# Down projection of an encoder block: operand parts kept in item order, a fresh accumulator for the last product, three weight loads traced earlier, the last block's products moved to VectorE

## The chip, the core and the metric

The kernel runs on one core of one Trainium2 chip. A core has a matrix engine (TensorE, PE in the profile, with PEld for its weight loads), VectorE (DVE), ScalarE (ACT), GpSimd (POOL) and a queue engine (SyncE, SP, SPq for its DMA issues). Matrix products land in an accumulator memory (PSUM), everything else is worked on in SBUF. The metric is the device time of one execution in microseconds (us). Time before: 1780.49 us, the median of 3 runs (1779.59 to 1781.81).

## The reference

One encoder layer is applied to two token groups of 256 and 512 tokens (768 rows of 1024 channels in all), with the same weights and in float32. Three token mixers (a state-space model, a differential attention, a cross-attention) are merged and projected, and a gated feed-forward network follows. Only its last line matters here:

```
h2 = rmsnorm(x, ffn_norm_g[li])
g, up = jnp.split(h2 @ w_gate_up[li], 2, axis=-1)
x = x + (jax.nn.silu(g) * up) @ w_down[li]
```

`w_gate_up` is 1024 x 5632, `w_down` is 2816 x 1024. The last matrix product, (768 x 2816) by (2816 x 1024), and the addition to `x` are the down projection.

## The kernel before

**Three matmuls for one.** A float32 operand is split into a high part (ScalarE copies it to a rounded format) and a low part (VectorE subtracts the high part from the original). `mm3` (lines 748 to 753) then issues three matmuls: high by high, high by low, low by high. `split_evac` (line 739) makes the two parts of an operand; with a `scale` it multiplies on the way.

**The blocks ahead of the down projection.** The hidden dimension is worked off in 11 feature blocks `fb` of 256 columns, each with a "gate" and an "up" half (`block`, line 1437). A block makes seven products of half size (Strassen-Winograd form), each of 12 matmuls on 384 columns; `plus` adds products up on VectorE, and a `fin` finishes each of four output quarters: `fin_gate` (tanh on ScalarE, then VectorE) or `fin_up`, which multiplies the gate by the up value. `fin_up` runs on GpSimd in these blocks (`kw`, line 1463). `hid_store` (line 1425) writes the finished hidden block to DRAM (`hid_scr`). `hook` is called only in the last "up" block, right after its first product is copied; it is `down_early`, which loads and prepares the first operands of the down projection.

**The down projection** is again a Strassen-Winograd product, over halves of the tokens (`r`, 384 rows), of the hidden dimension (`kh`) and of the output columns (`f`, 512 wide). It has seven products in the order P2, P1, P5, P6, P3, P7, P4. Each is cut into NG = 6 granules along the hidden dimension, five of two 128-row slices and one of a single slice. A pair (product, granule) is an item; there are 42, numbered from 0 (P2 is items 0 to 5, P1 6 to 11, P5 12 to 17, and so on). An item of two slices has 18 matmuls of 512 columns (three token tiles of 128 rows, two slices, three matmuls each), the single-slice item 9, and a product 99. Per item:

- `w_fetch(i)` brings the weights. P2, P3 load a quarter of `w_down` into a raw buffer (`dwr`), P1 into one of six long-lived tiles `ch[g]` (`dch` in the profile), all on the SP queue. P5, P6 and P4 work on `ch[g]` too: a GpSimd DMA adds another quarter to it in place (line 1752). P7 loads `dwt` tiles and adds a quarter to them in the same way.
- `a_load` (line 1725) brings hidden values from `hid_scr` (`da`), again on SP. Twelve of them, for the two quarters that P5 to P7 use, are asked for at P5's items.
- `make(i)` turns them into parts: the weights' high and low part (`whd` line 742, `wld` line 743), for P5, P6, P3 and P7 an addition or subtraction of two hidden quarters (`tt`, recorded at line 1765, the subtraction of P5 in place in `da`), and the token operand's high and low part (`dxh` line 745, `dxl` line 746). Four buffers hold weight parts and three hold token parts.
- then the item's matmuls, and after a product's last item three additions of the accumulators into the residual rows `x1` (line 1840, `x<-x,dn`), and for some products the store of the finished rows.

The loop makes item i + 2 before the matmuls of item i, fetches weights six and hidden values seven items ahead.

**Accumulators.** Tiles in two groups of PSUM buffers, "d" (five) and "b" (three). P2 has three fresh d tiles, P1 three fresh b tiles, P5 three fresh d tiles. P6, P7 and P4 go on adding to P1's b tiles and P3 to P5's d tiles: the Winograd chain sums are made in PSUM. So the first matmul of P4 on a tile comes after P7's addition has read that tile.

**What sets the order.** Instructions are traced in program order, but the queue of each engine is put in order by a planner that simulates the kernel at build time: an instruction goes to its engine when the planner believes its inputs to be there. The waits on the chip are semaphores that follow data and buffers, and an engine takes its queue in order. `pin`, that is `keep_in_program_order`, fixes an instruction behind the one traced just before it on the same engine (whatever that is, pinned or not). Before, the down projection's loads on SP and its adding loads on GpSimd are pinned, and nothing on ScalarE and VectorE is.

Of the kernel before, what the change touches and what calls it, by code (L numbers as in the profile page):

```python
# [8 lines left out]
F32 = mybir.dt.float32  # L9
F32R = mybir.dt.float32r  # L10
I32 = mybir.dt.int32
AF = mybir.ActivationFunctionType
# [614 lines left out]
def hybrid_block(ctx, tc, A, outs, consts):  # L627
    nc = tc.nc
    v, act, gp, pe = nc.vector, nc.scalar, nc.gpsimd, nc.tensor
    mul, add, sub = ALU.mult, ALU.add, ALU.subtract  # L630
# [17 lines left out]
    def uid(s):  # L648
        cnt[0] += 1
        return f"{s}_{cnt[0]}"  # L650
# [85 lines left out]
    def mean_eps(x, n, d):  # L736
        v.tensor_scalar(out=x, in0=x, scalar1=1.0 / d, scalar2=1e-6, op0=mul, op1=add)

    def split_evac(hi, lo, src, scale=None):

        if scale is None:
            act.activation(hi, src, AF.Copy)
            v.tensor_tensor(out=lo, in0=src, in1=hi.bitcast(F32), op=sub)  # L743
        else:
            act.activation(hi, src, AF.Copy, scale=scale)
            v.scalar_tensor_tensor(out=lo, in0=src, scalar=scale, in1=hi.bitcast(F32), op0=mul, op1=sub)  # L746

    def mm3(ps, wh, wl, xh, xl, start, stop, more=False):

# [47 lines left out]
    def bcast_load(pool, ap, n, name):  # L797
        t = pool.tile([128, n], F32, name=name)
        nc.sync.dma_start(t, ap.unsqueeze(0).to_broadcast([128, n]))
        return t  # L800
# [168 lines left out]
    D, P3 = {}, {}  # L969
    mrs2 = k1.tile([128, 4], F32, name="mrs2")  # L970
    with tc.tile_pool(name="nrm", bufs=1) as pool, tc.tile_pool(name="nrmg", bufs=1) as pg:
# [4 lines left out]
        ps = env.psa("gT")  # L976
# [9 lines left out]
        for t0 in (0, 2):  # L986
            for k0 in range(0, 8, 2):
                ps = env.psb("nT")
# [16 lines left out]
        for t in range(4):  # L1005

            tc.keep_in_program_order(v.scalar_tensor_tensor(out=xm[t], in0=xm[t], scalar=1.0, in1=xm[t], op0=mul,
                                                            op1=mul, accum_out=mss[:, t : t + 1]))
# [6 lines left out]
        g = bcast_load(pg, A["norm_mix_g"][0], 1024, "gmix")  # L1015
# [84 lines left out]
    with ExitStack() as c2:  # L1100
# [4 lines left out]
        for c in range(12):  # L1105
            W.by_dma = True
            w = W.get()
            for m in range(2):
                M = 2 * c + m
                for sg, (c0, n) in enumerate(SEGS):  # L1110
                    gt = glp.tile([128, 512], F32, name=uid("glt"), tag="glt")
                    ps = psd("gl")
# [23 lines left out]
    for i, nme in enumerate(("diff_q_g", "diff_k_g")):  # L1136
        g = rp[:, 2, 64 * i : 64 * i + 64]
# [247 lines left out]
    with tc.tile_pool(name="gelu", bufs=1) as yp:  # L1385
        for m in range(2):
            gelu_load(m, yp)
        for j, h in enumerate(DIFF_HEADS):
# [3 lines left out]
            for n_v, u_ in enumerate(v_units(last // 2) if h is None else qk_units(h)):  # L1392
                n_unit += 1
                W.by_dma = n_unit >= LOADED and not final
                m, r = divmod(n_unit, GELU_UNITS)
# [4 lines left out]
                if final and n_v % 2:  # L1400

                    t = slice(128 * (n_v - 1), 128 * (n_v + 1))
# [24 lines left out]
    def new_block(what, fb):  # L1427
        if what == "gate":
            act_in[fb] = fa.tile([128, 2, TOK], F32, name=uid("fa"), tag="fa")
# [14 lines left out]
    def block(what, fb, hook=None):  # L1444

        new_block(what, fb)
        w = W.get()
        fin = fin_gate if what == "gate" else fin_up

        def prod(l, r):  # L1450
            ps = psd(what)[:, 0:HT]
            (wh, wl), (xh, xl) = w[l], R[r]
            for k in range(4):
                mm3(ps, wh[:, k], wl[:, k], xh[:, k], xl[:, k], k == 0, k == 3)
            return ps

        def plus(o, x, y):
            v.tensor_tensor(out=o, in0=x, in1=y, op=add)

        tmp = [stg.tile([128, TOK], F32, name=uid("fs"), tag="brr") for _ in range(2)]  # L1460
        h1, h2 = slice(0, HT), slice(HT, TOK)
        (c11, c12), (c22, c21) = ((t[:, h1], t[:, h2]) for t in tmp)
        kw = {} if what == "gate" else {"eng": gp}
        act.activation(c12, prod("A11", "B11"), AF.Copy)
        if hook:
            hook()
        plus(c11, c12, prod("A12", "B21"))
        fin(fb, c11, 0, h1, **kw)
        plus(c12, c12, prod("S2", "T2"))
        p5 = prod("S1", "T1")  # L1470
        plus(c21, c12, prod("S3", "T3"))
        plus(c22, c21, p5)
        plus(c12, c12, p5)
        fin(fb, c22, 1, h2, **kw)
        plus(c12, c12, prod("S4", "B22"))
        fin(fb, c12, 0, h2, **kw)
        plus(c21, c21, prod("A22", "T4"))
        fin(fb, c21, 1, h1, **kw)

    with ExitStack() as c5:  # L1480
# [64 lines left out]
        x1, XB, Z = L["x1"], L["XB"], L["Z"]  # L1545
        S = pair(XA, "s5o")
        for c in range(4):
            w = W.get()
            for m in range(2):
                M = 2 * c + m  # L1550
                t = gtp.tile([128, TOK], F32, name=uid("gt"), tag="glr")
                zs = stg.tile([128, TOK], F32, name=uid("zs"), tag="brr")
                gp.dma_start(zs, z_scr[M])
                for c0, n in SEGS:
                    ps = psd("glu")
# [18 lines left out]
        g = fnp.tile([128, 1024], F32, name="gffn", bufs=1)  # L1574
# [120 lines left out]
    P2, P1, P5, P6, P3, P7, P4 = range(7)  # L1695
    NG = NFB // 2 + 1

    def granule(kh, g):
        if g < NG - 1:
            return (NG - 1) * kh + g, 0, 2  # L1700
        return NFB - 1, kh, 1

    ITEMS = [(p, g) for p in range(7) for g in range(NG)]
    AHEAD, FETCH, LOAD = 2, 6, 7
    EARLY = 4
    pin = tc.keep_in_program_order
# [5 lines left out]
    DP, a_raw, ch, w_raw, parts = {}, {}, {}, {}, {}  # L1712
# [14 lines left out]
    def w_quarter(kh, f, g):  # L1727
        fb, m, n = granule(kh, g)
        return wd[:, 2 * fb + m : 2 * fb + m + n, 512 * f : 512 * f + 512]

    def w_fetch(i):

        if i >= len(ITEMS):
            return
        p, g = ITEMS[i]
        n = granule(0, g)[2]
        view = lambda t: t.rearrange("p (k c) -> p k c", k=2)[:, 0:n]
        acc = None
        if p in (P1, P5, P6, P4):
            if p == P1:  # L1740
                ch[g] = view(DP["ch"].tile([128, 1024], F32, name=f"dch{g}"))
                pin(nc.sync.dma_start(ch[g], w_quarter(0, 0, g)))
            else:
                acc = {P5: (0, 1), P6: (1, 1), P4: (1, 0)}[p]
            t = ch[g]
        else:
            t = view(DP["r"].tile([128, 1024], F32, name=f"dwt{i}", tag="dwt") if p == P7 else
                     W.praw.tile([128, W.HALF], F32, name=f"dwr{i}", tag="wr"))
            src, acc = {P3: ((1, 1), None), P7: ((0, 1), (1, 1)), P2: ((1, 0), None)}[p]
            pin(nc.sync.dma_start(t, w_quarter(*src, g)))  # L1750
        if acc:
            pin(gp.dma_start(t, w_quarter(*acc, g), accum_op=add))
        w_raw[i] = t

    def make(i):

        if i >= len(ITEMS):
            return
        p, g = ITEMS[i]
        n = granule(0, g)[2]  # L1760
        t = w_raw.pop(i)
        wh, wl = (x.rearrange("p (k c) -> p k c", k=2)[:, 0:n] for x in W.tiles(f"d{i}"))
        split_evac(wh, wl, t)
        A_ = lambda r, kh: a_raw[(r, kh), g]
        tt = lambda o, x, y, op: v.tensor_tensor(out=o, in0=x, in1=y, op=op)
        sign = 0.5
        s_ = A_(1, 0) if p in (P5, P6, P3, P7) else None
        if p == P1:
            x = A_(0, 0)
        elif p == P5:  # L1770
            x = s_
            tt(x, x, A_(1, 1), sub)
        elif p == P6:
            x = s_
            tt(x, x, A_(0, 0), sub)
        elif p == P3:
            x = DP["t"].tile([128, 2, HT], F32, name=uid("ds4"), tag="ds4")[:, 0:n]
            tt(x, s_, A_(0, 1), add)
        elif p == P7:
            x = s_  # L1780
            tt(x, x, A_(1, 1), add)
            sign = -0.5
        else:
            x = A_(*((0, 1) if p == P2 else (1, 1)))
        xh, xl = (da_f.tile([128, 2, HT], F32R, name=uid("dx" + w), tag="dx" + w)[:, 0:n] for w in "hl")
        split_evac(xh, xl, x, sign)
        parts[i] = xh, xl, wh, wl

    def item_loads(i):
# [19 lines left out]
    xbctx.close()  # L1809

    with ExitStack() as c7:
        for k, n in (("a", 1), ("ch", 1), ("t", 2), ("r", 3)):
            DP[k] = c7.enter_context(tc.tile_pool(name="down" + k, bufs=n))
        HOME = {P1: (0, 0, add), P5: (1, 1, add), P6: (0, 1, sub), P3: (0, 1, add), P7: (1, 1, sub),
                P2: (0, 0, add), P4: (1, 0, add)}
        acc = {}
        for i in range(EARLY, LOAD):
            item_loads(i)
        for i in range(AHEAD + 3, FETCH):
            w_fetch(i)  # L1820
        for i, (p, g) in enumerate(ITEMS):
            item_loads(i + LOAD)
            w_fetch(i + FETCH)
            make(i + AHEAD)
            bank = "b" if p in (P1, P6, P7, P4) else "d"
            if g == 0 and p in (P1, P5, P2):
                acc[bank] = [PS[bank].tile([128, 512], F32, name=uid("dn"), tag=bank) for _ in range(3)]
            ps = acc[bank]
            n = granule(0, g)[2]
            xh, xl, wh, wl = parts.pop(i)  # L1830
            for t in range(3):
                c = slice(128 * t, 128 * t + 128)
                for k in range(n):
                    mm3(ps[t], xh[:, k, c], xl[:, k, c], wh[:, k], wl[:, k],
                        g == 0 and k == 0 and p in (P1, P5, P2), g == NG - 1 and k == n - 1, p in (P6, P3, P7, P4))
            if g == NG - 1:
                r, f, op = HOME[p]
                for t in range(3):
                    o = x1[3 * r + t][:, 512 * f : 512 * f + 512]
                    v.tensor_tensor(out=o, in0=o, in1=ps[t], op=op)  # L1840
                    if p in (P1, P3, P7, P4):
                        nc.sync.dma_start(os_[3 * r + t][:, 512 * f : 512 * f + 512], o)
    de.close()
# [44 lines left out]
```

## Time and profile before

| what | value |
|---|---|
| median of 3 runs | 1780.49 us (1779.59 to 1781.81) |
| the profiled execution's own time | 1780.2 us |
| its span, first to last instruction | 1778.4 us |
| mean granted TensorE clock | 0.994 of full speed |
| PE busy, PE weight loads busy | 1747.6 us (98%), 1613.2 us (91%) |
| DVE, ACT, POOL busy | 1265.1, 888.0, 282.2 us |
| down projection's first and last matmul start | 1606.2 and 1773.9 us |

The profile is a page of one execution with the span cut into views: the list of waits (who waited for whom, in all, how often, the longest), stretches (busy time of every engine with the number of instructions, the granted TensorE clock and the share of the 16 DMA engines), and the timeline of an engine (start, duration, line, operation, output and inputs; in brackets the engine's idle time just before and what ended it). The granted clock is 1.00 at full speed. Busy time of PE alone says little, as its matmuls overlap; the pitch from start to start is what counts.

### The profile page before, as it was taken

To read this page: it belongs to the slowest core of one execution; us is meant where nothing else is said; L and a number is where in the kernel's file an instruction comes from. 1 tells how busy PE (TensorE), PEld (TensorE's weight loads), DVE (VectorE), ACT (ScalarE), POOL (GpSimd) and SP (SyncE) were. 2 spreads that over 40 slices of the span, in tenths; PEclk is the share of its full clock that TensorE was granted. 3 is DMA by queue.
4 is the path that set the end of the run, shared out by engine and by line. 5 is a ranking of instruction groups with operands and counts; after the bars stand their busy time and mean duration, and the time that the engine had idled before them with its cause. 6 is when DMAs were issued, how large, how long until landed. Compare 5 with 4: busy or idle time off the path is not lost.

```text
span 1778.4 us, 29418 instructions
## 1 busy us (share of the span) xinstructions
PE 1747.6 (98%) x11194; PEld 1613.2 (91%) x11194; DVE 1265.1 (71%) x2342; ACT 888.0 (50%) x1856; POOL 282.2 (16%) x300
## 2 busy tenths in 40 slices
PE   9999999999999999999989999999999999999998
PEld 9999988999999999999979888888889999997786
DVE  6765658699999689788866435353598777774874
ACT  6444434677676356877756434232343333343342
POOL 0000000000000101110110002000136565541211
PEclk9999999999999999999999999999999999999999
DMA  7222745655656466543773336331312333338865
GB/s 257 82 84 96 139 112 117 179 136 139 154 134 159 130 156 163 117 91 90 161 175 98 120 124 245 113 116 65 90 62 93 107 94 112 97 134 258 188 156 122
DMA packets 209661, 234.09 MB, mean 132 GB/s; under 512 B 57832, under 2 KB 173296, under 8 KB 209520
## 3 DMA queue, kind: packets, MB, share of 16 engines
q1 hardware_dynamic: 184080, 164.05, 30.5%
q0 software_dynamic: 24288, 65.02, 17.2%
q10 hardware_dynamic: 1152, 3.15, 0.5%
q8 instruction: 88, 1.44, 0.3%
q14 instruction: 53, 0.43, 0.1%
HBM read 165.78 MB, written 41.22 MB: 116 GB/s over the span
## 4 chain that ended last, share of the span: by engine, by line
PE 55%; DMA 4%; DVE 2%; issue 1%; SPq 1%; ACT 0%; POOL 0%; ACTq 0%; DVEq 0%; POOLq 0%
PE br L751 4%; PE br L752 4%; PE br L753 4%; PE gate L751 3%; PE gate L753 3%; PE up L753 3%; PE gate L752 3%; PE up L752 3%; PE up L751 3%; PE dn L753 2%; PE dn L751 2%; PE dn L752 2%; PE av L1311 2%; PE qk L752 2%; PE qk L751 2%; PE qk L753 2%
## 5 line engine op out<-in xcount | busy, mean ns | idle before, releaser
L595 ACT ACTIVATE wh<-wr 128x1024 fp32r<-128x1024 f32 x124 | 140.6, 1133 | 73.1 <-PE br L752 30.2
L601 DVE TENSOR_TENSOR wl<-wr,wh 128x1024 fp32r<-128x1024 f32 x82 | 108.5, 1325 | 84.8 <-ACT wh L595 82.9
L751 PE MATMUL gl<-Hhi,wh 128*128 128x256 f32 (+1 forms) x384 | 132.4, 345 | 2.3 <-ACT glt L1114 2.3
L753 PE MATMUL gl<-Hhi,wl 128*128 128x256 f32 (+1 forms) x384 | 129.0, 336 | 0.0
L752 PE MATMUL gl<-Hlo,wh 128*128 128x256 f32 (+1 forms) x384 | 128.7, 335 | 0.0
L752 PE MATMUL qk<-wl,Hhi 128*128 128x256 f32 x384 | 109.1, 284 | 0.0
L751 PE MATMUL qk<-wh,Hhi 128*128 128x256 f32 x384 | 108.8, 283 | 0.4 <-ACT V L1210 0.4
L753 PE MATMUL qk<-wh,Hlo 128*128 128x256 f32 x384 | 108.6, 283 | 0.0
L599 POOL DMA_DIRECT2D wl<-wr x42 | 36.6, 872 | 453.2 <-ACT wl L598 428.6
L752 PE MATMUL dn<-wld,dxh 128*128 128x512 f32 x231 | 90.6, 393 | 3.3 <-DVE wld L743 3.3
L751 PE MATMUL dn<-whd,dxh 128*128 128x512 f32 x231 | 90.7, 393 | 2.0 <-DVE x L1840 2.0
L753 PE MATMUL dn<-whd,dxl 128*128 128x512 f32 x231 | 89.8, 395 | 1.9 <-DVE dxl L746 1.9
L751 PEld LDWEIGHTS gl<-Hhi,wh 128*128 128x128 f32 x384 | 72.3, 188 | 9.7 <-ACT glt L1114 2.7
L753 PEld LDWEIGHTS gl<-Hhi,wl 128*128 128x128 f32 x384 | 72.0, 188 | 8.0
L752 PEld LDWEIGHTS gl<-Hlo,wh 128*128 128x128 f32 x384 | 72.2, 188 | 7.2
L1280 DVE TENSOR_REDUCE nm<-sc 128x1 f32<-128x512 f32 (+1 forms) x96 | 56.6, 598 | 28.0 <-PE sc L1275 27.0
L751 PEld LDWEIGHTS qk<-wh,Hhi 128*128 128x128 f32 x384 | 73.1, 190 | 1.5 <-ACT V L1210 0.6
L557 ACT ACTIVATE wh_S<-ws 128x512 fp32r<-128x512 f32 x70 | 41.1, 626 | 65.5 <-PE up L752 36.9
L753 PEld LDWEIGHTS qk<-wh,Hlo 128*128 128x128 f32 x384 | 73.3, 191 | 0.3
L752 PEld LDWEIGHTS qk<-wl,Hhi 128*128 128x128 f32 x384 | 72.8, 190 | 0.6
L558 DVE TENSOR_TENSOR wl_S<-ws,wh_S 128x512 fp32r<-128x512 f32 x70 | 57.9, 851 | 15.9 <-ACT wh_S L557 15.9
L1282 ACT ACTIVATE p<-sc,nm 128x512 f32<-128x512 f32 (+1 forms) x96 | 59.1, 620 | 17.5 <-DVE nm L1280 17.0
(478 smaller groups left out, 6016.5 us busy)
## 6 DMA issues: line engine op xcount, KB each, us to landing
wr<-in_w_in_dram SPq DMA_DIRECT2D x48, 512.0 KB, 4.6
wr<-in_w_gate_up_dram SPq DMA_DIRECT2D x44, 512.0 KB, 3.5
wl<-wr POOLq DMA_DIRECT2D x42, 512.0 KB, 5.2
wr<-in_w_branch_dram SPq DMA_DIRECT2D x24, 512.0 KB, 3.9
glr<-gl_scr POOLq DMA_DIRECT2D x24, 384.0 KB, 3.5
hid_scr<-fa SPq DMA_DIRECT2D x11, 768.0 KB, 6.3
wr<-in_w_mem_kv_dram SPq DMA_DIRECT2D x16, 512.0 KB, 3.6
wr<-in_w_in_dram SPq DMA_DIRECT2D x32, 256.0 KB, 4.7
```

What stands on the lines that cost most here:

```text
L557: self.nc.scalar.activation(f(hi), src, AF.Copy)
L558: self.nc.vector.tensor_tensor(out=f(lo), in0=src, in1=f(hi).bitcast(F32), op=ALU.subtract)
L595: self.nc.scalar.activation(hi, r, AF.Copy)
L599: self.nc.gpsimd.dma_start(lo, r.bitcast(F32R), accum_op=ALU.add)
L601: self.sub.tensor_tensor(out=lo, in0=r, in1=hi.bitcast(F32), op=ALU.subtract)
L751: pe.matmul(ps, wh, xh, start=start, stop=False, **kw)
L752: pe.matmul(ps, wh, xl, start=False, stop=False, **kw)
L753: pe.matmul(ps, wl, xh, start=False, stop=stop, **kw)
L1280: v.tensor_reduce(out=nm[:, m : m + 1], in_=ps, axis=AX.X, op=ALU.max, negate=True)
L1282: act.activation(pm[:, 0:n], ps, AF.Exp, bias=nm[:, m : m + 1], accum_out=s1s[:, tt : tt + 1] if m == 0 else s2)
L1311: pe.matmul(po[:, 0:128], aT[:, 128 * k : 128 * k + 128], V[:, c0 // 128 + k, 128 * (h % 2) : 128 * (h % 2) + 128], start=(k == 0), stop=( ...
```

## The change

Five edits, all but the last two lines within the down projection and its lead-in:

1. `split_evac` takes a `pin`, and `make` pins all that it issues on ScalarE and VectorE: weight parts, sums of hidden quarters, token parts.
2. P4 gets three fresh d tiles (`FRESH`) and no longer adds to the b chain. To make up for it, P7's end adds each b tile to a second set of residual rows as well (`o2`): three more VectorE additions.
3. The weight loads of P1's first three granules (items 6 to 8) are traced before the hidden loads of items 4 to 6 and are not pinned; later ones stay where they were, pinned.
4. The pools of the down projection are opened in another order (`ch` last), so `ch` lies on other memory that was used before it.
5. In the last "up" block (the one with a hook) `fin_up` runs on VectorE, not on GpSimd.

```
-    def split_evac(hi, lo, src, scale=None):
+    def split_evac(hi, lo, src, scale=None, pin=lambda i: i):
         if scale is None:
-            act.activation(hi, src, AF.Copy)
-            v.tensor_tensor(out=lo, in0=src, in1=hi.bitcast(F32), op=sub)
+            pin(act.activation(hi, src, AF.Copy))
+            pin(v.tensor_tensor(out=lo, in0=src, in1=hi.bitcast(F32), op=sub))
...
-        kw = {} if what == "gate" else {"eng": gp}
+        kw = {} if what == "gate" or hook else {"eng": gp}
...
-                pin(nc.sync.dma_start(ch[g], w_quarter(0, 0, g)))
+                load = nc.sync.dma_start(ch[g], w_quarter(0, 0, g))
+                if g > 2:
+                    pin(load)
...
-        split_evac(wh, wl, t)
+        split_evac(wh, wl, t, pin=pin)
-        tt = lambda o, x, y, op: v.tensor_tensor(out=o, in0=x, in1=y, op=op)
+        tt = lambda o, x, y, op: pin(v.tensor_tensor(out=o, in0=x, in1=y, op=op))
...
-        split_evac(xh, xl, x, sign)
+        split_evac(xh, xl, x, sign, pin)
...
-        for k, n in (("a", 1), ("ch", 1), ("t", 2), ("r", 3)):
+        for k, n in (("a", 1), ("t", 2), ("r", 3), ("ch", 1)):
...
+        FRESH = (P2, P1, P5, P4)
         acc = {}
+        for i in range(NG, NG + 3):
+            w_fetch(i)
         for i in range(EARLY, LOAD):
             item_loads(i)
...
-            w_fetch(i + FETCH)
+            if i + FETCH >= NG + 3:
+                w_fetch(i + FETCH)
             make(i + AHEAD)
-            bank = "b" if p in (P1, P6, P7, P4) else "d"
-            if g == 0 and p in (P1, P5, P2):
+            bank = "b" if p in (P1, P6, P7) else "d"
+            if g == 0 and p in FRESH:
                 acc[bank] = [PS[bank].tile([128, 512], F32, name=uid("dn"), tag=bank) for _ in range(3)]
...
                     v.tensor_tensor(out=o, in0=o, in1=ps[t], op=op)
+                    if p == P7:
+                        o2 = x1[3 + t][:, 0:512]
+                        v.tensor_tensor(out=o2, in0=o2, in1=ps[t], op=add)
```

More of the change, by code (lines that the diff above doesn't have):

```diff
@@ L737, in mean_eps @@
         v.tensor_scalar(out=x, in0=x, scalar1=1.0 / d, scalar2=1e-6, op0=mul, op1=add)
-    def split_evac(hi, lo, src, scale=None):
+    def split_evac(hi, lo, src, scale=None, pin=lambda i: i):
         if scale is None:
-            act.activation(hi, src, AF.Copy)
-            v.tensor_tensor(out=lo, in0=src, in1=hi.bitcast(F32), op=sub)
-        else:
-            act.activation(hi, src, AF.Copy, scale=scale)
-            v.scalar_tensor_tensor(out=lo, in0=src, scalar=scale, in1=hi.bitcast(F32), op0=mul, op1=sub)
+            pin(act.activation(hi, src, AF.Copy))
+            pin(v.tensor_tensor(out=lo, in0=src, in1=hi.bitcast(F32), op=sub))
+        else:
+            pin(act.activation(hi, src, AF.Copy, scale=scale))
+            pin(v.scalar_tensor_tensor(out=lo, in0=src, scalar=scale, in1=hi.bitcast(F32), op0=mul, op1=sub))
     def mm3(ps, wh, wl, xh, xl, start, stop, more=False):
@@ L1834, in hybrid_block @@
                     mm3(ps[t], xh[:, k, c], xl[:, k, c], wh[:, k], wl[:, k],
-                        g == 0 and k == 0 and p in (P1, P5, P2), g == NG - 1 and k == n - 1, p in (P6, P3, P7, P4))
+                        g == 0 and k == 0 and p in FRESH, g == NG - 1 and k == n - 1, p not in FRESH)
             if g == NG - 1:
```

## The prediction

> **What bounds the kernel now.** The page comes first, then the list of waits from 1600 us to the end, where the change lies.
>
> ```profile
> span 1778.4 us, 29418 instructions
> PE 1747.6 (98%) x11194; PEld 1613.2 (91%) x11194; DVE 1265.1 (71%) x2342; ACT 888.0 (50%) x1856; POOL 282.2 (16%) x300
> ...
> PE dn L752 <- DVE wld L743: 3.3, 1, 3.3
> PE dn L751 <- DVE x L1840: 2.0, 1, 2.0
> PE dn L753 <- DVE dxl L746: 1.9, 1, 1.9
> ```
>
> TensorE is the bound, and in the down projection it idles three times. Two things are to be known: what these stops cost in pitch, and what ended them. First the pitch, by stretches (behind POOL's column stand the granted clock, the DMA share and GB/s) and by PE's timeline:
>
> ```profile
> 1640.00:1645.00 5.00, 1.65 (x7) 0.93 (x5) 2.09 (x2) 1.86 (x3) 0.12 (x1) 1.00 1.07 353
> 1645.00:1652.00 7.00, 5.06 (x13) 3.93 (x13) 6.64 (x8) 0.13 (x1) 3.19 (x3) 0.51 1.09 317
> 1652.00:1700.00 48.00, 48.00 (x212) 39.20 (x211) 37.84 (x44) 21.71 (x26) 6.92 (x6) 1.00 0.64 138
> 1748.00:1752.00 4.00, 1.95 (x9) 1.34 (x8) 2.73 (x4) 2.67 (x3) 0.00 (x0) 1.00 1.13 206
> ...
> L751 PE MATMUL dn<-whd,dxh x231: 387/389/632, 1606.2 to 1773.5; 128*128 128x512 f32 x116
> ...
> 1640.90 0.39 PE L751 MATMUL dn<-whd,dxh 128*128 128x512 f32 x1
> 1644.63 0.49 PE L752 MATMUL dn<-wld,dxh 128*128 128x512 f32 x1 [3.35 <-DVE wld L743]
> 1647.07 0.80 PE L753 MATMUL dn<-whd,dxl 128*128 128x512 f32 x1 [1.94 <-DVE dxl L746]
> ...
> 1651.90 0.40 PE L752 MATMUL dn<-wld,dxh 128*128 128x512 f32 x1
> ...
> 1749.15 0.39 PE L753 MATMUL dn<-whd,dxl 128*128 128x512 f32 x1
> 1751.59 0.47 PE L751 MATMUL dn<-whd,dxh 128*128 128x512 f32 x1 [2.05 <-DVE x L1840]
> ```
>
> Undisturbed, 212 matmuls take 48.00 us: 0.2264 us each, 4.08 us for an item of 18, 22.4 us for a product of 99. Starting at 1606.2, P1's item 9 is due after 99 + 54 matmuls, at 1606.2 + 153 x 0.2264 = 1640.84: the first of its matmuls starts at 1640.90, so there was no loss up to there.
>
> From 1640.90 to 1651.90 stand 13 matmuls (the 12 between them each one row of the timeline), which would take 2.94 us and take 11.00: **8.06 us lost**. Of that 2.3 is the clock, 0.51 in this stretch: the 11 pitches from 1647.07 on take 4.83 for 2.49. From 1749.15 to 1751.59 one pitch takes 2.44 us: **2.21 us lost**, with the clock at 1.00. Against the whole: from the first start of line 751 to its last, 1606.2 to 1773.5, are 690 pitches or 156.2 us, so 11.1 were lost, 10.3 of them in these two places.
>
> Now what ended the first stop. These are ScalarE's and VectorE's timelines:
>
> ```profile
> 1630.69 1.06 ACT L742 ACTIVATE whd<-dch 128x1024 fp32r<-128x1024 f32 x1 [0.60 <-DMA dch<-in_w_down_dram]
> 1632.71 0.85 ACT L745 ACTIVATE dxh<-da 128x768 fp32r<-128x768 f32 x1 [0.96 <-PE dn L752]
> 1636.39 1.06 ACT L742 ACTIVATE whd<-dch 128x1024 fp32r<-128x1024 f32 x1 [2.83 <-DMA dch<-in_w_down_dram]
> 1643.14 0.63 ACT L742 ACTIVATE whd<-dch 128x512 fp32r<-128x512 f32 x1 [4.95 <-DMA dch<-in_w_down_dram]
> ...
> 1642.48 0.96 DVE L1765 TENSOR_TENSOR da<-da,da 128x768 f32<-128x768 f32 x1 [9.60 <-DMA da<-hid_scr]
> 1643.36 1.22 DVE L743 TENSOR_TENSOR wld<-dch,whd 128x1024 fp32r<-128x1024 f32 x1
> 1645.19 0.96 DVE L1765 TENSOR_TENSOR da<-da,da 128x768 f32<-128x768 f32 x1 [0.61 <-DMA da<-hid_scr]
> 1646.06 0.95 DVE L746 SCALAR_TENSOR_TENSOR dxl<-da,dxh 128x768 fp32r<-128x768 f32 x1
> ```
>
> Item 9's high parts were there at 1631.75 and 1633.56. Its `wld` could have run then; it ran at 1643.36, because VectorE's queue had P5's subtraction (items 12 and 13, needed 10 us later) ahead of it, waiting 9.60 us for a transfer. It is an order of one queue, not a lack of data.
>
> **The change, part by part.**
>
> *Pinned parts.* With VectorE's queue in item order, item 9's `wld` and `dxl` follow 1633.6 and end by 1636 (1.22 + 0.95 us), 4.8 us ahead of the need at 1640.9. Item 10: high part at 1637.45, done by 1640, need 1644.9. Item 11 (half size): weights landed at 1643.14, parts by about 1645.2, need 1649.0. P5's first item: its transfers had landed at 1642.48; subtraction, high part and low part take 0.96 + 0.85 + 0.95 us, so about 1647, need 1651.0. Even with every transfer as late as before nothing stops: the term is 8.06 us, the half clock with it. The price is that three additions at each product's end must now precede the `wld` three items on. Each takes 0.68 us, and that `wld` is needed 8.2 us after the product's end; nothing, except at the last change of product.
>
> *Fresh tiles for P4.* The wait for P7's additions goes: 2.21 us. What is late next are P4's own parts, made from weights that GpSimd adds last. Their chain, by the four engines:
>
> ```profile
> 1727.85 1.22 DVE L743 TENSOR_TENSOR wld<-dwt,whd 128x1024 fp32r<-128x1024 f32 x1
> 1728.99 0.68 DVE L1840 TENSOR_TENSOR x<-x,dn 128x512 f32<-128x512 f32 x1
> ...
> 1729.09 0.59 SPq L1750 DMA_DIRECT2D dwt<-in_w_down_dram  x1
> ...
> 1737.38 0.90 POOL L1752 DMA_DIRECT2D dwt<-in_w_down_dram  x1 [8.01 <-DMA dwt<-in_w_down_dram]
> ...
> 1745.16 1.06 ACT L742 ACTIVATE whd<-dch 128x1024 fp32r<-128x1024 f32 x1 [2.95 <-DMA dch<-in_w_down_dram]
> 1748.53 1.06 ACT L742 ACTIVATE whd<-dch 128x1024 fp32r<-128x1024 f32 x1 [1.57 <-DMA dch<-in_w_down_dram]
> ...
> 1749.62 1.23 DVE L743 TENSOR_TENSOR wld<-dch,whd 128x1024 fp32r<-128x1024 f32 x1 [1.27 <-ACT whd L742]
> 1750.76 0.68 DVE L1840 TENSOR_TENSOR x<-x,dn 128x512 f32<-128x512 f32 x1
> ```
>
> P7's third `wld` (1727.85) frees a `dwt` buffer, SP reloads it, GpSimd adds to it and only then starts P4's six additions; the first lands at 1745.16, the second at 1748.53. Parts take 1.06 + 1.23 + 0.95 = 3.2 us more: 1748.4 and 1751.8, against needs at 1749.4 and 1753.5. Both ends of the new cost: nothing, if VectorE takes P4's second item before P7's additions. Or the pin puts that 1727.85 behind P3's last addition (about 0.6 us), and six additions of 0.68 (4.1 us, three of them new) stand ahead of P4's second item from 1749: its `wld` then ends at 1754.3 and its `dxl` at 1755.2, some 1.3 us after the need. The first item's margin, 1.0 us, bears the 0.6. I take 0.5, nearer to nothing, since the item is traced before the additions.
>
> *Loads traced earlier, pools, fins.* These rows show the lead-in (GpSimd, then SP, then a stretch):
>
> ```profile
> 1606.54 2.98 POOL L1422 TENSOR_TENSOR fa<-fa,fs 128x384 f32<-128x384 f32 x2 [1.62 <-DVE fs L1458]
> ...
> 1607.60 0.53 SPq L1725 DMA_DIRECT2D da<-hid_scr  x1
> 1609.55 0.34 SPq L1425 DMA_DIRECT2D hid_scr<-fa  x1
> 1613.21 0.96 SPq L1725 DMA_DIRECT2D da<-hid_scr  x2
> ...
> 1615.44 0.59 SPq L1742 DMA_DIRECT2D dch<-in_w_down_dram  x1
> ...
> 1602.00:1606.00 4.00, 4.00 (x25) 4.00 (x24) 3.97 (x6) 1.06 (x1) 1.01 (x1) 1.00 0.45 131
> 1606.00:1610.00 4.00, 4.00 (x19) 3.33 (x19) 2.29 (x4) 1.06 (x1) 2.98 (x2) 1.00 0.22 60
> 1638.00:1642.00 4.00, 3.29 (x15) 2.40 (x13) 0.00 (x0) 0.18 (x1) 0.00 (x0) 1.00 1.09 271
> ```
>
> The first `dch` load stood behind the store of the last hidden block and the load that reads it back. Ahead of both it runs in stretches whose DMA share is 0.45 and 0.22, and 3 x 512 KB leave the stretch that is full (1.09); at its 271 GB/s they are 5.8 us of it. P1's first item is due at 1628.6, so none of it is on PE's path: zero, and a margin for the first part. Every later SP load is pinned behind the third of these loads; if its buffer frees only when the last block's products end (1606), the next load, which went at 1607.60, is not held. Four `fin_up` on VectorE cost about 2.2 us at the 0.55 us of its 384-column additions and take two GpSimd ones of 2.98 us off the store's path. VectorE is full from 1602 to 1606, but the pin sends P2's third `wld` behind the last fin, to about 1608; its item is due at 1606.2 + 36 x 0.2264 = 1614.4. Zero again.
>
> **The sum**, against the profiled execution's 1780.2 us (span 1778.4 and 1.8 around it): -8.06 - 2.21 + 0.5 = -9.8, so 1770.4. The median of the runs lies 0.3 above that execution, which I split: 1770.5.
>
> [...] The clock stood at 0.51 after 3.35 and 1.94 us of idling with one matmul between them, and at 1.00 after a single 2.05. [...]
>
> **The rivals.**
>
> *Transfers become the limit in P1 and P5.* GpSimd's addition to `ch` for P5's fourth granule waits for item 9's `wld`; it now starts 10 us sooner, and so do the next two, 1.25 MB in the stretch whose DMA share is already 1.09. At 271 GB/s and twice the traffic for an addition that delays the last P1 weights or P5's hidden values by up to 9 us; 5.8 us come back from the moved loads, and their margins are about 4. A residue of 2 to 5 us stays: 1772.5 to 1775.5. [...]
>
> *P4's parts replace P4's wait.* The upper end of the second part and the 0.6 on top of it: 2 us back, 1772.0.
>
> *The order does not change where it matters,* for instance because an unpinned addition takes the place of the subtraction ahead of `wld`: 1780. Against it: item 9's parts precede P5's in the trace, and each is tied to the one before.
>
> *Slower: the pin holds VectorE for a transfer.* Nothing may pass P5's first subtraction any more. If its hidden values land after about 1648, each further us stops TensorE; slower by 0.2% begins at 10 + 3.6 us beyond, a landing at 1662 or later, and a stop so long halves the clock as well, so some 1659 would do: 1784. For it speaks the DMA share, against it that these transfers landed at 1642.48 with more bytes ahead of them.
>
> **How the numbers follow.** Both stops go: 0.64. Transfers limit: 0.13. P4's parts: 0.06. No change of order: 0.07. Slower: 0.10. 0.2% (3.6 us) is about what a measurement here tells from nothing; so faster is 0.83, same 0.07, slower 0.10. The range holds the first three: from 1769.0 (all 10.3 us and a little of the other pitch) to 1776.0.
>
> **What would show it.** No PE wait on `wld` or `dxl` near 1640, clock 1.00 from 1606 on, P5's subtractions behind P1's last `dxl` on VectorE; no PE wait on `x` before P4, at most about 1 us on its second item; last matmul near 1764. The prediction is wrong if a PE wait on a part whose transfer came late stands between P1 and P5, or if P2 starts late.

## The result and the profile after

The changed kernel takes 1774.09 us (median of 22 runs, 1771.07 to 1778.71), the kernel before in the same comparison 1777.39 us (1774.46 to 1783.24). The ratio is 0.9979, 95% interval 0.9970 to 0.9987: 2.3 to 5.3 us faster, by the ratio 3.7. The forecast was 9.8 us faster. The range held the time and the sign was right, but well over half of the expected gain is missing.

The page of the kernel after:

```profile
span 1772.3 us, 29415 instructions
...
PE 1743.5 (98%) x11194; PEld 1609.4 (91%) x11194; DVE 1268.0 (72%) x2349; ACT 887.5 (50%) x1856; POOL 277.0 (16%) x296
```

Its list of PE's waits (us in all, times, longest) over the whole execution, cut to the down projection:

```profile
PE dn L751 <- ACT dxh L745: 4.8, 4, 2.7
PE dn L753 <- DVE dxl L746: 0.6, 1, 0.6
```

None of the three old stops in the down projection is left: no wait on `wld` or on `x`, and the one on `dxl` is another (1720.05 below). A new one leads the whole list: PE waits for `dxh`, four times. The stretches of the kernel after say where (columns as in the prediction):

```profile
1636.00:1652.00 16.00, 16.00 (x73) 13.24 (x72) 10.98 (x14) 5.07 (x6) 3.70 (x4) 1.00 1.11 248
1652.00:1694.00 42.00, 42.00 (x187) 34.80 (x186) 30.21 (x36) 18.25 (x22) 4.12 (x4) 1.00 0.54 139
1694.00:1744.00 50.00, 44.65 (x190) 34.84 (x189) 35.28 (x40) 19.54 (x24) 14.14 (x12) 1.00 0.81 182
1744.00:1768.00 24.00, 24.00 (x107) 19.71 (x105) 14.95 (x20) 7.78 (x10) 0.00 (x0) 1.00 0.36 82
```

The matmuls of line 751, with their first and last start, from the view of one tile:

```profile
L751 PE MATMUL dn<-whd,dxh x231: 387/389/504, 1603.7 to 1767.4; 128*128 128x512 f32 x116
```

And PE's timeline, the rows with an idle time:

```profile
1698.97 0.50 PE L751 MATMUL dn<-whd,dxh 128*128 128x512 f32 x1 [1.15 <-ACT dxh L745]
1717.82 0.50 PE L751 MATMUL dn<-whd,dxh 128*128 128x512 f32 x1 [0.16 <-ACT dxh L745]
1720.05 0.50 PE L753 MATMUL dn<-whd,dxl 128*128 128x512 f32 x1 [0.58 <-DVE dxl L746]
1732.22 0.50 PE L751 MATMUL dn<-whd,dxh 128*128 128x512 f32 x1 [0.72 <-ACT dxh L745]
1739.34 0.50 PE L751 MATMUL dn<-whd,dxh 128*128 128x512 f32 x1 [2.75 <-ACT dxh L745]
```

The stretch with the old first stop now holds 73 matmuls in 16 us at full clock. The new losses lie in P3 and P7, between 1694 and 1744. A measure for all that follows: line 751's starts are 690 pitches apart, 156.2 us undisturbed. Before they took 167.3, so 11.1 us were lost in the stage; here they take 163.7, so 7.5 are lost. The stage gained 3.6 us, which is what the ratio says. (The two profiled executions differ by 6.1; the other 2.5 lie ahead of the stage, and are taken up at the end.)

So 10.3 us of old stops went, as forecast, and about 7 us of new ones came (190 matmuls in the 50 us from 1694, which would take 43.0). What makes `dxh` late? ScalarE's timeline at P3:

```profile
1698.07 0.84 ACT L745 ACTIVATE dxh<-ds 128x768 fp32r<-128x768 f32 x1 [4.74 <-DVE ds L1767]
1698.82 1.04 ACT L742 ACTIVATE whd<-dwr 128x1024 fp32r<-128x1024 f32 x1
1702.10 0.85 ACT L745 ACTIVATE dxh<-ds 128x768 fp32r<-128x768 f32 x1 [2.24 <-DVE ds L1767]
```

And VectorE's:

```profile
1694.68 1.28 DVE L1846 TENSOR_TENSOR x<-x,dn 128x512 f32<-128x512 f32 x2
1695.87 1.22 DVE L743 TENSOR_TENSOR wld<-dwr,whd 128x1024 fp32r<-128x1024 f32 x1
1697.01 0.95 DVE L1767 TENSOR_TENSOR ds<-da,da 128x768 f32<-128x768 f32 x1
1698.95 0.96 DVE L746 SCALAR_TENSOR_TENSOR dxl<-ds,dxh 128x768 fp32r<-128x768 f32 x1 [0.99 <-ACT dxh L745]
1699.90 1.22 DVE L743 TENSOR_TENSOR wld<-dwr,whd 128x1024 fp32r<-128x1024 f32 x1
1701.04 0.95 DVE L1767 TENSOR_TENSOR ds<-da,da 128x768 f32<-128x768 f32 x1
```

Read them as one chain. ScalarE does `dxh` of one item (1698.07) and, next in its pinned order, `whd` of the next (1698.82, to 1699.86). VectorE's pinned order then has that item's `wld` (1699.90), and behind it the sum of hidden quarters (`ds`, 1701.04). The sum is the input of the next `dxh`, which starts at 1702.10. One turn takes 4.03 us, and an item on PE 4.08. (There is a second way round: `dxl` stands ahead of that `wld` in VectorE's queue and ends at 1699.91, beside `whd`. Both ways go through `wld` ahead of the sum.) Both engines wait for each other in turn (ScalarE 2.24, VectorE 0.99 us) while neither is busy all the time, and no lead that is lost comes back. The additions at a product's end (`x`, 1694.68, 1.28 us for two) cost such a lead.

P7 pays twice, since its weights are reloaded into a buffer that a `wld` frees. Its second `wld` in VectorE's timeline, the reload in SP's, the late `whd` in ScalarE's:

```profile
1719.92 1.22 DVE L743 TENSOR_TENSOR wld<-dwt,whd 128x1024 fp32r<-128x1024 f32 x1
```

```profile
1721.16 4.38 SPq L1752 DMA_DIRECT2D dwt<-in_w_down_dram  x2
```

```profile
1735.14 1.06 ACT L742 ACTIVATE whd<-dwt 128x1024 fp32r<-128x1024 f32 x1 [2.97 <-DMA dwt<-in_w_down_dram]
```

P7's first matmul is at 1717.82, so this `wld` comes 2 us after it. The reload behind it, with GpSimd's addition to it, lands at 1735.1, and PE idles 2.75 us ahead of 1739.34.

### The profile page after: what moved, and what is told of

Its sections match the earlier page's. It is cut to its first block, busy times and chain, and to the rows that moved or that the text cites. A ratio compares the mean times of both kernels' runs of the same rounds, so it can differ in the third digit from the quotient of the medians.

```text
span 1772.3 us, 29415 instructions
## 1 busy us (share of the span) xinstructions
PE 1743.5 (98%) x11194; PEld 1609.4 (91%) x11194; DVE 1268.0 (72%) x2349; ACT 887.5 (50%) x1856; POOL 277.0 (16%) x296
## 4 chain that ended last, share of the span: by engine, by line
PE 57%; DMA 3%; DVE 2%; issue 1%; ACT 1%; POOL 0%; SPq 0%; ACTq 0%; POOLq 0%; DVEq 0%
PE br L751 3%; PE br L752 3%; PE br L753 3%; PE gate L751 3%; PE gate L753 3%; PE up L753 3%; PE gate L752 3%; PE up L752 3%; PE up L751 3%; PE dn L751 3%; PE dn L752 3%; PE dn L753 3%; PE av L1311 2%; PE qk L752 2%; PE qk L751 2%; PE qk L753 2%
## 5 line engine op out<-in xcount | busy, mean ns | idle before, releaser
L753 PE MATMUL dn<-whd,dxl 128*128 128x512 f32 x231 | 82.0, 390 | 0.6 <-DVE dxl L746 0.6
```

What stands on the lines that cost most here:

```text
L753: pe.matmul(ps, wl, xh, start=False, stop=stop, **kw)
```

## The experiments

Three theories for the new loss. *Loop*: the chain just read, closed by the pins. *Ends*: the additions at a product's end, which the planner put ahead of the next parts, where they wait for PE. *Transfers*: P7's weights late for reasons of their own. The ratios below are to the kernel before; "lost" is line 751's spread less 156.2 us.

**Sums first.** `make` traces the sum before the weights' parts, so its pin no longer puts it behind `wld`:

```
-        split_evac(wh, wl, t, pin=pin)
         A_ = lambda r, kh: a_raw[(r, kh), g]
...
+        split_evac(wh, wl, t, pin=pin)
         split_evac(xh, xl, x, sign, pin)
```

> Edit: in make, the pinned sum of hidden quarters is traced before the weights' parts instead of after them. Three theories for the 7.5 us that the changed kernel still loses between the down projection's matmuls (from P3 on, PE waiting for dxh). Loop: ScalarE's queue holds dxh of one item before whd of the next, VectorE's holds wld of an item before its sum, and dxh waits for the sum; so dxh, whd, wld, sum, dxh follow each other across two queues, 4.03 us per item (ScalarE's dxh at 1698.07, 1702.10, 1706.14), against 4.08 on PE, and a lead once lost isn't made up. With the sum first the loop is dxh, dxl, sum, dxh, some 2.7 us: the waits on dxh go, under 1 us stays lost, ratio to before about 0.994. Ends: the additions at a product's end, which stand in VectorE's queue ahead of the next parts and wait for PE, are the cause: they still do, 1.3 us in P3 and more than 4 us in all stay lost, ratio about 0.997. Transfers: P7's reloaded weights come late for their own reasons: the 2.9 us before its fifth item stay, ratio about 0.996.

Measured: 1768.44 us, ratio 0.9948 (0.9932 to 0.9965). Line 751 of this kernel, the stretch of P3 and P7, and then the same place in ScalarE's and in VectorE's timeline:

```profile
L751 PE MATMUL dn<-whd,dxh x231: 387/389/390, 1606.7 to 1763.2; 128*128 128x512 f32 x116
```

```profile
1694.00:1744.00 50.00, 50.00 (x222) 41.40 (x222) 34.61 (x41) 21.14 (x25) 14.10 (x12) 1.00 0.82 184
```

```profile
1701.99 0.85 ACT L745 ACTIVATE dxh<-ds 128x768 fp32r<-128x768 f32 x1 [1.07 <-DVE ds L1766]
1704.87 0.85 ACT L745 ACTIVATE dxh<-ds 128x768 fp32r<-128x768 f32 x1 [1.08 <-PE dn L753]
```

```profile
1700.06 0.95 DVE L746 SCALAR_TENSOR_TENSOR dxl<-ds,dxh 128x768 fp32r<-128x768 f32 x1
1700.92 0.95 DVE L1766 TENSOR_TENSOR ds<-da,da 128x768 f32<-128x768 f32 x1
1701.79 1.22 DVE L743 TENSOR_TENSOR wld<-dwr,whd 128x1024 fp32r<-128x1024 f32 x1
```

Lost: 0.3 us, and no wait of PE in the stage. The sum (1700.92) now stands ahead of `wld` (1701.79); the next `dxh` follows 2.9 us later, waiting for PE to free its buffer and for nothing on VectorE. With the same instructions in another order, this kernel beats both others: its interval and that of the changed kernel (0.9970 to 0.9987) don't meet. VectorE is as busy between 1694 and 1744 as in the changed kernel (34.61 against 35.28 us), and P7's transfers were cured with it.

**Ends pinned.** The changed kernel with the additions pinned, so that they stand behind the parts two items ahead:

```
-                    v.tensor_tensor(out=o, in0=o, in1=ps[t], op=op)
+                    pin(v.tensor_tensor(out=o, in0=o, in1=ps[t], op=op))
...
-                        v.tensor_tensor(out=o2, in0=o2, in1=ps[t], op=add)
+                        pin(v.tensor_tensor(out=o2, in0=o2, in1=ps[t], op=add))
```

> Edit: the changed kernel with the additions at a product's end pinned too, so they follow the parts of the item two ahead in VectorE's queue. Ends: with them out of the way the waits go, under 1 us lost, ratio about 0.994. Loop: still 4.03 us per item and about 3 us for the half-sized one that PE does in 2.04, so the lead grows by the additions' 1.9 us once and drains on; the loss in P3 goes or shrinks, 3 to 5 us stay lost, mostly in P7, ratio about 0.9965. Transfers: 2.9 us in P7 stay, ratio about 0.996.

Measured: 1773.44 us, ratio 0.998 (0.9971 to 0.999). Line 751, PE's wait on `dxh` in its list, and five starts of `dxh` in ScalarE's timeline:

```profile
L751 PE MATMUL dn<-whd,dxh x231: 387/389/504, 1602.3 to 1764.9; 128*128 128x512 f32 x116
```

```profile
PE dn L751 <- ACT dxh L745: 3.4, 5, 1.3
```

```profile
1694.37 0.85 ACT L745 ACTIVATE dxh<-ds 128x768 fp32r<-128x768 f32 x1 [2.24 <-DVE ds L1767]
1700.12 0.84 ACT L745 ACTIVATE dxh<-ds 128x768 fp32r<-128x768 f32 x1 [3.95 <-DVE ds L1767]
1704.15 0.85 ACT L745 ACTIVATE dxh<-ds 128x768 fp32r<-128x768 f32 x1 [2.24 <-DVE ds L1767]
1708.19 0.85 ACT L745 ACTIVATE dxh<-ds 128x768 fp32r<-128x768 f32 x1 [2.24 <-DVE ds L1767]
1711.22 0.53 ACT L745 ACTIVATE dxh<-ds 128x384 fp32r<-128x384 f32 x1 [1.66 <-DVE ds L1767]
```

Lost: 6.4 us, hardly less than 7.5 and more than I gave the loop. Ends falls: out of the way, the additions still cost their time in the loop, and the turn with all three in it took 5.75 us (1694.37 to 1700.12). Transfers falls too, as PE's longest wait is 1.3 us and not 2.9. A turn is 4.04 us for a full item and 3.03 for the half one, which PE does in 2.04, so each product drains the lead by about another microsecond.

**One more addition, in the loop and out of it.** To tell a loop from plain load, VectorE got the same extra addition per summed item in two kernels: the changed one, where it lies between `wld` and the sum, and the one with sums first. Its result is not used.

```
+        if s_ is not None:
+            junk = DP["t"].tile([128, 2, HT], F32, name=uid("djk"), tag="djk", bufs=1)[:, 0:n]
+            tt(junk, s_, s_, add)
         if p == P1:
```

> Edit: the changed kernel with one more addition on VectorE (0.87 us of its time, result unused) between wld and the sum of each of the 24 items that have a sum. Loop: the loop takes 4.03 + 0.87 = 4.9 us per item against 4.08 on PE; about 0.8 us per full item and 1.4 per half one on top of the 7.5 us already lost, less what lead is left: 20 to 28 us lost in the stage. Load (VectorE's work as such, about 2.9 us per item and 1.9 per product's end, becomes 3.75, 22.7 per product of 22.4): 1 to 3 us on top, 9 to 11 lost.

> Edit: the same extra addition, in the kernel with the sums first. VectorE does the same work as in the run beside it. Loop: dxh, dxl, extra, sum, dxh makes 2.7 + 0.87 = 3.6 us per item, under PE's 4.08: less than 2 us lost. Load: as much on top as in the run beside it.

Measured: 1787.86 us in the loop and 1770.17 us with the sums first, one run each. Line 751 of the first, one turn in its ScalarE's timeline, line 751 of the second, and a stretch of the first and the same of the second (PE, PEld, then VectorE):

```profile
L751 PE MATMUL dn<-whd,dxh x231: 387/389/632, 1602.6 to 1781.1; 128*128 128x512 f32 x116
```

```profile
1711.94 0.84 ACT L745 ACTIVATE dxh<-ds 128x768 fp32r<-128x768 f32 x1 [3.11 <-DVE ds L1767]
1716.84 0.84 ACT L745 ACTIVATE dxh<-ds 128x768 fp32r<-128x768 f32 x1 [3.11 <-DVE ds L1767]
```

```profile
L751 PE MATMUL dn<-whd,dxh x231: 387/389/504, 1604.5 to 1763.4; 128*128 128x512 f32 x116
```

```profile
1694.00:1716.00 22.00, 18.66 (x77) 14.12 (x78) 18.74 (x23) 7.52 (x10) 0.57 (x1) 1.00 0.39 120
```

```profile
1694.00:1716.00 22.00, 21.61 (x96) 17.57 (x95) 21.90 (x27) 10.06 (x12) 3.64 (x3) 1.00 0.75 188
```

A turn grew from 4.03 to 4.90 us, by just the addition, and 22.3 us were lost. With the sums first the same work lost 2.7 us, more than the less than 2 expected: VectorE is busy for 21.90 of 22 us there, an estimated 22.7 per product of 22.4, so here load shows as well. In the loop it is less busy (18.74) and the loss is far greater. The 20 us between the two come of the order alone.

**Sums free.** The changed kernel with the parts pinned and the sums not:

```
-        tt = lambda o, x, y, op: pin(v.tensor_tensor(out=o, in0=x, in1=y, op=op))
+        tt = lambda o, x, y, op: v.tensor_tensor(out=o, in0=x, in1=y, op=op)
```

> Edit: the changed kernel with the sums of hidden quarters left unpinned, parts pinned. If the pin on the sums is what took P1's stop away, the stop is back: the planner has put P5's first sum ahead of the wld of P1's third item, waiting for its transfer, and 5 to 12 us are lost there, half clock with it, ratio 0.998 to 1.002. The waits in P3 and P7 go under the loop theory, since the sums run ahead again. If the pins on the parts alone do it, under 2 us are lost and the ratio is 0.995.

Measured: 1773.12 us, ratio 0.9976 (0.9964 to 0.9988). Line 751, then the stop on VectorE and on PE:

```profile
L751 PE MATMUL dn<-whd,dxh x231: 387/389/628, 1609.6 to 1771.1; 128*128 128x512 f32 x116
```

```profile
1637.64 0.96 DVE L1767 TENSOR_TENSOR da<-da,da 128x768 f32<-128x768 f32 x1 [8.67 <-DMA da<-hid_scr]
```

```profile
1640.12 0.50 PE L753 MATMUL dn<-whd,dxl 128*128 128x512 f32 x1 [3.14 <-DVE dxl L746]
```

Lost: 5.3 us, all in P1; this stop is the only wait of PE in the stage, and P3 and P7 lose nothing. The pin on the sums is both the cure of P1 and, where it stands, the illness of P3 and P7.

**Pins alone,** on the kernel before (the diff of `split_evac` and `make` only, as in the change):

> Edit: the kernel before with the pins alone. All theories: the stop in P1 (8.06 us) goes and the stop before P4 (2.2 us) stays. Loop and ends: the new losses in P3 and P7 come with the pins, so 8 to 10 us are lost in the stage against 11.05 before, ratio 0.999. If the moved loads, the pools or the fins on VectorE made the new losses, they aren't here: 3 us lost, ratio 0.9955.

**Fresh tiles alone,** on the kernel before (`FRESH`, `bank` and the `o2` additions only):

> Edit: the kernel before with the fresh tiles for P4 alone. The stop before P4 goes and the one in P1 stays: 11.05 - 2.3 = 8.8 us lost, ratio 0.9987. If P4's own parts are late (my rival), up to 2 us of it come back at P4's second item, ratio 0.9998.

**The change without its lead-in, sums first:** the kernel before with pins and fresh tiles as in the change and the sums traced first, without the loads traced earlier, the order of pools and the fins on VectorE:

> Edit: the kernel before with the pins (sums first) and the fresh tiles for P4, but without the loads traced earlier, the other order of pools and the fins on VectorE. My step costed these three at nothing: no PE wait in the down projection, under 1 us lost, ratio as with sums first, 0.9945. If the transfers moved ahead are what keeps P1 and P5 fed (my first rival turned round), PE waits for whd or dxh in P1 or P5 and 2 to 5 us are lost, ratio 0.996 to 0.998.

Measured, in this order: 1776.76 us, ratio 0.9992 (0.9977 to 1.0006); 1776.22 us, ratio 0.9988 (0.9977 to 0.9999); 1768.48 us, ratio 0.9946 (0.9930 to 0.9961). Line 751 and one row of PE's timeline, its last wait in the stage, first of the kernel with pins alone, whose wait on `dxh` in PE's list stands last:

```profile
L751 PE MATMUL dn<-whd,dxh x231: 387/389/504, 1605.1 to 1770.1; 128*128 128x512 f32 x116
```

```profile
1748.24 0.47 PE L751 MATMUL dn<-whd,dxh 128*128 128x512 f32 x1 [1.19 <-DVE x L1840]
```

```profile
PE dn L751 <- ACT dxh L745: 3.7, 6, 1.3
```

Of the kernel with fresh tiles alone:

```profile
L751 PE MATMUL dn<-whd,dxh x231: 387/389/629, 1604.7 to 1769.3; 128*128 128x512 f32 x116
```

```profile
1644.56 0.80 PE L753 MATMUL dn<-whd,dxl 128*128 128x512 f32 x1 [2.95 <-DVE dxl L746]
```

Of the last:

```profile
L751 PE MATMUL dn<-whd,dxh x231: 387/389/402, 1602.2 to 1759.8; 128*128 128x512 f32 x116
```

```profile
1742.39 0.50 PE L753 MATMUL dn<-whd,dxl 128*128 128x512 f32 x1 [0.60 <-DVE dxl L746]
```

Pins alone lose 8.8 us: P1's stop is gone, P4's stays, and the new losses are there (six waits on `dxh`) without any other part of the change, so the pins make them. Fresh tiles alone lose 8.4: P1's stop stays and P4's is gone. The last loses 1.4 us, and its ratio is that of the kernel with the whole lead-in: the loads traced earlier, the pools and the fins together are worth nothing that the ratios show (in the stage, by one profiled execution of each, 1.1 us). Its one wait in the stage stands at P4's second item, where the prediction looked for it.

## Why the prediction was right and where it was wrong

- *P1's stop, 8.06 us, an order and not a lack of data: right.* It went in every kernel that pins the sums and stayed in both experiments that don't, and no transfer came late: after the change P5's first subtraction waited for no transfer.
- *The price of the pins, "nothing, except at the last change of product": wrong, and this is the step that failed.* It measured about 7 us. I laid out the times of item 9 to P5's first item, found margins of 4 to 5 us, and took them to hold for every item: the `wld` "is needed 8.2 us after the product's end". That is true only if the parts keep their lead. I priced each engine's queue by itself, where 3 us of VectorE's work per item stand against 4.08 on PE, and did not follow the way from one `dxh` through both queues to the next. Its length could be read from rows that I had: 0.85 + 1.06 + 1.22 + 0.96 us, 4.1 in all, as long as an item on PE.
- *"The pin puts that 1727.85 behind P3's last addition (about 0.6 us)": same step, too small.* That `wld`, P7's third, came some 1.5 us behind P7's first matmul before (by the pitch, that matmul is at 1726.4) and 6.1 us behind it after the change (1723.94 against 1717.82); the second ran 4 us ahead of it before and 2 us behind it after.
- *P4's stop, 2.21 us: right.* Its own parts (0.5 us, between 0 and 1.3): 0.75 us in the kernel without the lead-in, nothing in the changed kernel or with sums first and the lead-in. The size was fair.
- *Loads traced earlier, pools, fins, all at zero: right* as far as the ratios tell, by the last experiment.
- *The rivals.* The transfers of P1 and P5 did not become the limit, and the pin never held VectorE for a late one. "Twice the traffic for an addition" is about what it costs in time: before, from 1575 to 1660, the packets of the queue with GpSimd's additions took 19.4% of the 16 engines' span for 3.00 MB and those of the queue with SP's loads 54.8% for 15.99 MB, per MB 1.9 times as much. The time lies in the range of the rival on transfers (1772.5 to 1775.5), but for another reason, and with 6.1 us of the forecast gain missing, not 2 to 5; the true mechanism was on no list, and of the signs named only the last matmul was off (1767.8, not near 1764).
- *That the time lies in the forecast range is luck.* The range was set from a time before of 1780.5, of 3 runs; over 22 runs it is 1777.4. Set from that, 3.1 us lower, it would have ended at 1772.9, short of 1774.09.

The two terms of the gain, then, were right, and a cost put at zero, of a mechanism that the prediction did not see, ate two thirds of them. With the sum traced ahead of the weights' parts the kernel gains about what the sum in the prediction said: by the ratio 9.2 us (6.2 to 12.1), against 9.8.

## What to carry to other kernels

Before queues are pinned, follow one item's parts through all engines to the same point of the next item: if that way leads from one pinned queue into another and back, its length is a rate, and it must lie clearly below the rate of the engine to be fed, at the half-sized items and product ends too. In a pinned order put first what the other engine waits for (here the sum), not what it has just delivered. And a margin found at one item is a margin only if the feeding chain is faster than its user; at 4.03 against 4.08 us a lead is spent once.

## What the runs showed beyond that

The span of single profiled executions says less than the stage. The instructions ahead of the last block stand in the same order before and after, yet the first down matmul starts at 1606.2 us before and at 1603.7 after, and the experiments' starts scatter from 1602.2 to 1609.6. One source can be read: the stretch from 900 to 920, before and then after, with the granted clock third from the right:

```profile
900.00:920.00 20.00, 16.19 (x101) 14.35 (x100) 6.16 (x15) 6.30 (x22) 0.00 (x0) 0.91 0.63 156
```

```profile
900.00:920.00 20.00, 16.35 (x110) 14.58 (x109) 7.67 (x22) 8.91 (x30) 0.00 (x0) 1.00 0.56 139
```

The clock dropped in one and not in the other, behind the same wait of 2.6 us. In the execution before, it was halved from 911.2 to 914.6 and, behind P1's stop of 3.35 and 1.94 us, from 1645.0 to 1651.9, for 3.41 and for 6.83 us, and the two drops lie 733.9 us apart, 215 times 3.413. In the traces of the kernels before and after, all changes of the clock lie a whole number of such steps apart.

The length of a wait alone did not tell whether the clock halved. Of PE's other waits of 2 us and more in these two executions, those of 2.09 and 2.13 us (before; ended at 665.58 and 1006.03) and of 2.10, 2.12 and 2.41 us (after; 665.11, 1003.28 and 306.63) have a drop of 3.41 us beside them. Those of 2.05 and 2.29 us (before; 1751.59 and 308.19) and of 2.75 us (after; 1739.34) have none. The 2.05 us are P4's stop, the 2.75 us P7's; 2.29 and 2.41 us were waited for the same part of the program.

For changes of a few microseconds the lost time inside the stage was the better scale: 11.1 - 7.5 = 3.6 us against 3.7 by the ratio of 22 runs. In the experiments with a ratio the two lie 0.1 to 1.6 us apart, each time inside the ratio's interval.
